# RMS norms in an interleaved attention/retention trunk: sums as rows through split products with ones

## The chip, the cores and the metric

The kernel runs on one core of one Trainium2 chip. The metric is the device time of one execution in microseconds (us); the median of three runs before the change is 2588.68 us (2587.34 to 2588.96). The engines are named as in the profile: PE is the matrix engine (PEld its weight loads), DVE the vector engine, ACT the scalar engine, POOL the GpSimd engine, SP the queue that issues most DMAs.

## The reference

Two layers, each a token mixer and a feed-forward block, every one behind an RMS norm and added to the residual; a last RMS norm ends it. x is 1 x 1024 tokens x 1024 features, float32.

```
def rmsnorm(x, g):
    y = x * rsqrt(mean(x * x, axis=-1, keepdims=True) + EPS)      # EPS = 1e-6
    return y * g

for i in range(2):
    h = rmsnorm(x, norm_mix[i])
    x = x + (forgetting_attention(h) if i == 0 else retention(h))
    h = rmsnorm(x, norm_ffn[i])
    x = x + swiglu(h)                   # (silu(h @ Wg) * (h @ Wu)) @ Wo, d_ff = 2816
return rmsnorm(x, final_norm)
```

The forgetting attention has 8 heads of 128 and a causal softmax with a decay bias. The retention has 4 heads with 256 query/key and 512 value features; its output y of every head and token is normalised before a gate: (y - mean(y)) * rsqrt(var(y) + EPS), over the head's 512 features, then times silu(g), then the output projection.

## The kernel before, in words

**Layout.** Everything is kept transposed: features on the 128 partitions, tokens in the free dimension, in two halves of 512 tokens (`HALF`). A float32 operand of a product is split into a high part, cast by ACT, and a low part, the rest, subtracted by DVE (`split`, L97 to L99); a product is then three matmuls hi*hi, hi*lo, lo*hi (`mm_u`, L101 to L108; `Products.run`, L645 to L647). The feed-forward layers, the projections of retention and part of the output projections run in a seven-product scheme on 2 x 2 blocks (`Products`, `in_turn`, `paired_out`), the operand sums (`T1` to `T4`) of which are made beforehand: `Combos` holds them in SBUF, `Stored` puts those of the feed-forward activations into DRAM (`ac...`) and fetches them back (`landed`, L496: a DMA on SP's queue straight into the low part's buffer, then a split there).

**The norms.** `Norm` accumulates the squares of the 8 feature tiles into `acc` (128 x 512 for each half; each row of it still holds one partition's share). What remains is a sum over the partitions. `colsum` (L156) takes `acc` as the stationary operand, 128 tokens at a time, against one column of a tile of ones: tokens land on partitions, four columns for a half. On these columns of 4 elements `rsqrt` (L142) takes ACT's root, DVE's reciprocal and one Newton step. To multiply tiles whose tokens lie in the free dimension, `rows` (L162) then broadcasts each column over all partitions, by a matmul of the column, repeated 128 times, with the identity. `rms` (L169) does both for the two halves and copies the result to `R` (128 x 1024). Both kinds of matmul are plain float32 ones, and each stands in the trace as two instructions. All their results, and the next column sum, go through one bank of PSUM, `ms`.

`rms` is called four times: before the attention (its columns also scale the values and keys), in each feed-forward layer's first use of R (L835) and in the first gate product of retention (L976; its columns make `kap` and `rho`, the factors of keys and outputs with their decays). `finish` (L1130) normalises a retention block of one head and one half, eight times in all: column sum of `acc`, small operations with `rho`, `rsqrt`, `rows`, then four output tiles times that row block, a gate for head 0, and the stores to `zd`. The final norm (L873 to L892) is done in three pieces of 512, 256 and 256 tokens, each ending in `colsum`, `rsqrt`, `rows`, eight multiplies and eight stores.

**Order.** The program is written for a scheduler that orders each engine's instructions in program order as priority, moving a later one ahead when earlier ones are not ready; each engine then runs its list strictly in that order. In retention the scores of the next block are made while the present one is weighted with its values: `scores` (L1080) ends in DVE steps (L1100, L99, L1105) whose results `weighted` (L1109) multiplies one block later. Pools bound how far work can run ahead: 16 tiles `y` of 128 x 512, five staging tiles `st` of 128 x 1024, six pairs `wh`/`wl` of split weights, seven PSUM banks for products and the bank `ms`.

**The joints of the feed-forward layer.** While the last of the 22 gate products runs, `coming` makes each finished block of products fetch operands of the first stored group (`FROM_COMBOS`); while the last product of group 0 runs, those of group 1 are fetched the same way (`FROM_STORED`). The start of the kernel loads four weight tiles of the first head's keys (256 KB), then the first x tiles, then the rest.

Of the kernel before, what the change touches and what calls it, by code (L numbers as in the profile page):

```python
# [37 lines left out]
def trunk(ctx, tc, nc, d, out):  # L38
# [12 lines left out]
    nc.scalar.dma_start(gains, d["gains"])  # L51
    R = cp.tile([P, S], F32, tag="R", name="R")
    cnt = [0]
# [47 lines left out]
    def mm_u(ps, wts, acts, h, cols=slice(0, H), first=True, last=True):  # L101
        n = len(wts)
        for k in range(n):
            wh, wl = wts[k]
            xh, xl = (t[:, cols] for t in acts[k][h])
            nc.tensor.matmul(ps, wh, xh, start=(first and k == 0), stop=False)  # L106
            nc.tensor.matmul(ps, wh, xl, start=False, stop=False)  # L107
            nc.tensor.matmul(ps, wl, xh, start=False, stop=(last and k == n - 1))  # L108
# [53 lines left out]
    def rows(col, mp, mtag, nb=4):  # L162
        ps = mp.tile([P, H], F32, tag=mtag, name=nm("rw"))
        for b in range(nb):
            nc.tensor.matmul(ps[:, b * P:(b + 1) * P], col[:, b:b + 1].to_broadcast([P, P]), ident,
                             start=True, stop=True)
        return ps

    def rms(norm, mp, mtag, halves=(0, 1)):  # L169
        rc = small([P, TB], "rcol", 2)  # L170
        for h in halves:
            ps = colsum(norm.acc[h], mp, mtag)
            v = small([P, 4], "rv")
            nc.vector.tensor_scalar(v, ps[:, 0:4], 1.0 / D, EPS, op0=ALU.mult, op1=ALU.add)
            rsqrt(v, 4, rc[:, 4 * h:4 * h + 4])
        for h in halves:
            ps = rows(rc[:, 4 * h:4 * h + 4], mp, mtag)
            nc.scalar.copy(R[:, HALF[h]], ps)
        return rc
# [5 lines left out]
    with ExitStack() as fs:  # L185
# [13 lines left out]
        wk0, wk1 = wtile(d["fox_qk"][1], 4), []  # L199
        for kt in range(KT):  # L200
            xs = []
            for h in range(2):
                t = half("t", 9)
                nc.sync.dma_start(t, d["xT"][:, kt, HALF[h]])
                xs.append(t)
            fed = norm.feed(kt, xs)
            x0.append(xs)
            for at, w, idx, k in (0, wk0, 1, 4), (1, wk1, 3, 0), (3, wk1, 3, 4):
                if kt == at:
                    w += wtile(d["fox_qk"][idx][:, k * P:], 4)  # L210
# [225 lines left out]
        rc = rms(norm, mp, "ms")  # L436
# [59 lines left out]
    def landed(pool, src):  # L496

        hi, lo = units(pool)
        nc.sync.dma_start(lo.bitcast(F32), src)
# [47 lines left out]
    FROM_COMBOS = {"S2": ("B11", "T1", "T2"), "S3": ("B21", "T3"), "S4": ("T4", "B22")}  # L547
# [3 lines left out]
    class Stored:  # L551


        def __init__(self, name, pools):
            self.pools = pools
# [114 lines left out]
    def in_turn(srcs, X, use, coming=None):  # L670
# [3 lines left out]
        for i in range(n):  # L674
# [7 lines left out]
            nxt = Products(srcs[i + 1], X, coming if i == n - 2 else None).open() if i < n - 1 else None  # L682
# [145 lines left out]
    def ffn(i, X, nrm, xold, xnew, last, nw, pools):  # L828
        ad = [dp.tile([P, S], F32, tag=f"ad{i}_{f}", name=f"ad{i}_{f}") for f in range(16, FT)]
        stored = [Stored(f"ac{i}_{g}_", pools) for g in range(2)]  # L830
        even = []

        def gated(f, c11, c12, c21, c22):
            if f == 0:
                rms(nrm, mp, "ms")  # L835
# [7 lines left out]
            if f < 16:  # L843
# [10 lines left out]
        in_turn([nw if f == 0 and nw else d["ffn_in"][i, f] for f in range(FT)], X, gated,  # L854
                (stored[0], FROM_COMBOS))
# [17 lines left out]
        for c0, c1 in ((0, 512), (512, 768), (768, 1024)):  # L873
# [3 lines left out]
            for n in range(KT):  # L877
                u = y[n][h][:, cs]
                ps = mm_ps()
                mm_u(ps[:, :wid], ws[n], acts, h, cs)  # L880
                nc.vector.tensor_tensor(u, ps[:, :wid], u, op=ALU.add)
                norm.square(h, u, cs, n == 0)
                nc.scalar.activation(u, u, AF.Copy, scale=gains[:, 4, n:n + 1])
                us.append(u)
            nb = wid // P
            ps = colsum(norm.acc[h][:, cs], mp, "ms", nb)
            v = small([P, nb], "rv")
            nc.vector.tensor_scalar(v, ps[:, 0:nb], 1.0 / D, EPS, op0=ALU.mult, op1=ALU.add)
            ps = rows(rsqrt(v, nb), mp, "ms", nb)
            for n in range(KT):  # L890
                nc.vector.tensor_tensor(us[n], us[n], ps[:, :wid], op=ALU.mult)
# [82 lines left out]
    def gates(p, c11, c12, c21, c22):  # L974
        if p == 0:
            rcs.append(rms(nrm, mp, "ms"))  # L976
# [33 lines left out]
    rho = small([P, RET_HEADS, TB], "rho", 1)  # L1010
    rho2 = small([P, RET_HEADS, TB], "rho2", 1)
    for h in range(RET_HEADS):
        nc.vector.tensor_tensor(kap[:, h, :], gpn[:, 0, h, :], r2, op=ALU.mult)
        nc.vector.tensor_tensor(rho[:, h, :], gpn[:, 1, h, :], rc, op=ALU.mult)
    nc.vector.tensor_tensor(rho2, rho, rho, op=ALU.mult)
# [114 lines left out]
    def finish(h, ib, yps):  # L1130
# [12 lines left out]
        cs = colsum(acc, mp, "ms")  # L1143
        var = small([P, 4], "yv")
        rs = slice(4 * ib, 4 * ib + 4)
        nc.vector.scalar_tensor_tensor(var, cs[:, 0:4], 1.0 / 512, rho2[:, h, rs], op0=ALU.mult, op1=ALU.mult)
        nc.vector.tensor_scalar(var, var, EPS, None, op0=ALU.add)
        r = rsqrt(var, 4)
        fac = small([P, 4], "yf")
        nc.vector.tensor_tensor(fac, r, rho[:, h, rs], op=ALU.mult)  # L1150
        fb = rows(fac, mp, "ms")
# [137 lines left out]
```

## Time and profile before

| | before |
|---|---|
| median of three runs | 2588.68 us |
| the profiled execution's own time | 2588.64 us |
| its span | 2586.9 us |
| PE busy | 2560.8 us, 12808 matmuls |
| DVE busy | 1839.0 us, 3131 instructions |
| ACT busy | 1228.3 us, 2320 instructions |
| POOL busy | 170.6 us, 147 instructions |
| TensorE clock granted | 0.998 |

The span is the time from the first to the last recorded instruction of the program. Rows of a line (L159 and so on) give the number of instructions, then shortest, median and longest duration in ns, first and last start in us, and shapes. A timeline row is start, duration, engine, line, operation, out<-in, and what ended an idle time before it. A row of a window gives its length and, for PE, PEld, DVE, ACT and POOL, busy us and instructions; then the clock, the DMA engines' share and GB/s. A wait's row gives who waited for whom: us in total, times, longest. Matmul durations hold their latency and overlap; what one costs PE is read from the next one's start.

### The profile page before, as it was taken

The page shows a single profiled execution, that of the slowest core. Times are in us where ns is not written, and L with a number is a line of the kernel's source. Part 1 is how long each engine was busy: PE and PEld are TensorE (multiplying, and loading weights), DVE is VectorE, ACT ScalarE, POOL GpSimd, SP SyncE. Part 2 cuts the span into 40 slices and gives each one's busy share as a digit, 9 for nine tenths or more (in the row PEclk, how much of TensorE's full clock was granted, in tenths as well). Part 3 has the DMA queues.
Part 4 walks back from the last instruction along what each step waited for, and adds up shares of the span by engine and source line. Part 5 has one row for each costly group of instructions (what it writes and reads, how often), then busy time and mean ns, then how long its engine had stood idle before and what let it go on. Part 6 is the DMA issues. An engine that isn't in the chain of part 4 may idle for free.

```text
span 2586.9 us, 35264 instructions
## 1 busy us (share of the span) xinstructions
PE 2560.8 (99%) x12808; PEld 2182.2 (84%) x12808; DVE 1839.0 (71%) x3131; ACT 1228.3 (47%) x2320; POOL 170.6 (7%) x147
## 2 busy tenths in 40 slices
PE   9999999999999999999999999999999999999998
PEld 8889887888888878889898989898888888888888
DVE  6798888966666678886656576785567666668784
ACT  6566656543333454554343435662354333335543
POOL 0143323000000000001000010000000000000000
PEclk9999999999999999999999999999999999999999
DMA  3111142432332345533332325555522333325541
GB/s 130 45 58 58 58 147 93 152 106 94 114 106 94 122 155 176 166 116 115 102 118 98 110 98 167 184 191 193 202 98 82 110 98 107 103 90 186 175 143 66
DMA packets 145759, 312.13 MB, mean 121 GB/s; under 512 B 16560, under 2 KB 29616, under 8 KB 145584
## 3 DMA queue, kind: packets, MB, share of 16 engines
q1 hardware_dynamic: 144864, 309.33, 35.9%
q8 instruction: 100, 1.64, 0.3%
q14 instruction: 75, 0.61, 0.1%
q10 hardware_dynamic: 720, 0.55, 0.1%
HBM read 217.54 MB, written 92.27 MB: 120 GB/s over the span
## 4 chain that ended last, share of the span: by engine, by line
PE 93%; DVE 2%; DMA 2%; issue 2%; ACT 1%; POOL 0%; SPq 0%; DVEq 0%; POOLq 0%; ACTq 0%
PE mm L645 18%; PE mm L647 18%; PE mm L646 18%; PE mm L106 7%; PE mm L107 7%; PE mm L108 7%; PE mm L765 2%; PE mm L763 2%; PE mm L764 2%; PE mm L256 1%; PE mm L257 1%; PE mm L258 1%; DMA b<-ac_T 1%; PE mm L1116 1%; PE mm L1117 1%
## 5 line engine op out<-in xcount | busy, mean ns | idle before, releaser
L645 PE MATMUL mm<-b,wh 128*128 128x512 f32 x2128 | 826.7, 390 | 2.7 <-ACT b L98 2.7
L646 PE MATMUL mm<-b,wh 128*128 128x512 f32 x2128 | 827.9, 389 | 0.0
L647 PE MATMUL mm<-b,wl 128*128 128x512 f32 x2128 | 825.2, 389 | 0.0
L98 ACT CAST wh<-st 128x512 fp32r<-128x512 f32 (+1 forms) x449 | 276.6, 617 | 499.2 <-PE mm L646 298.3
L645 PEld LDWEIGHTS mm<-b,wh 128*128 128x128 f32 x2128 | 399.4, 188 | 86.5 <-ACT b L98 4.0
L647 PEld LDWEIGHTS mm<-b,wl 128*128 128x128 f32 x2128 | 399.5, 188 | 83.2 <-DVE wl L99 0.4
L646 PEld LDWEIGHTS mm<-b,wh 128*128 128x128 f32 x2128 | 399.6, 188 | 82.1
L99 DVE TENSOR_TENSOR wl<-st,wh 128x512 fp32r<-128x512 f32 (+1 forms) x449 | 318.6, 713 | 180.3 <-ACT wh L98 177.9
L98 ACT CAST wh<-s 128x512 fp32r<-128x512 f32 x252 | 156.5, 622 | 298.5 <-PE mm L646 270.6
L106 PE MATMUL mm<-b,wh 128*128 128x512 f32 x736 | 286.8, 393 | 7.8 <-ACT b L126 5.5
L107 PE MATMUL mm<-b,wh 128*128 128x512 f32 x736 | 287.4, 391 | 1.7 <-DVE b L99 1.7
L108 PE MATMUL mm<-b,wl 128*128 128x512 f32 x736 | 287.4, 391 | 0.0
L99 DVE TENSOR_TENSOR wl<-s,wh 128x512 fp32r<-128x512 f32 x252 | 180.2, 717 | 89.6 <-ACT wh L98 85.5
L106 PEld LDWEIGHTS mm<-b,wh 128*128 128x128 f32 x736 | 138.9, 189 | 37.3 <-ACT b L126 6.2
L107 PEld LDWEIGHTS mm<-b,wh 128*128 128x128 f32 x736 | 138.9, 189 | 29.5 <-DVE b L99 2.2
L108 PEld LDWEIGHTS mm<-b,wl 128*128 128x128 f32 x736 | 138.8, 189 | 28.4
L764 PE MATMUL mm<-wl,b 128*128 128x256 f32 x448 | 126.6, 283 | 0.0
L763 PE MATMUL mm<-wh,b 128*128 128x256 f32 x448 | 126.2, 283 | 0.0
L765 PE MATMUL mm<-wh,b 128*128 128x256 f32 x448 | 126.2, 283 | 0.0
L597 DVE TENSOR_TENSOR s<-st 128x512 f32<-128x512 f32 x84 | 58.2, 692 | 67.8 <-DMA st<-ffn_in 28.8
L98 ACT CAST b<-b 128x512 fp32r<-128x512 f32 x112 | 67.7, 620 | 71.9 <-DMA b<-ac_B 39.2
L99 DVE TENSOR_TENSOR b<-b,b 128x512 fp32r<-128x512 f32 x112 | 75.5, 688 | 33.0 <-ACT b L98 32.6
(500 smaller groups left out, 4019.7 us busy)
## 6 DMA issues: line engine op xcount, KB each, us to landing
st<-ffn_in SPq DMA_DIRECT2D x88, 512.0 KB, 3.5
st<-ffn_out_pairs SPq DMA_DIRECT2D x32, 512.0 KB, 3.6
b<-ac_T SPq DMA_DIRECT2D x64, 256.0 KB, 5.8
ac_T<-t SPq DMA_DIRECT2D x48, 256.0 KB, 2.4
b<-ac_B SPq DMA_DIRECT2D x48, 256.0 KB, 5.0
st<-fox_qk SPq DMA_DIRECT2D x32, 256.0 KB, 2.7
xo<-xd SPq DMA_DIRECT2D x32, 256.0 KB, 3.0
ac_B<-t SPq DMA_DIRECT2D x32, 256.0 KB, 2.4
```

The source lines that it names most:

```text
L98: nc.scalar.copy(hi, src)
L99: return nc.vector.tensor_tensor(lo, src, hi.bitcast(F32), op=ALU.subtract)
L106: nc.tensor.matmul(ps, wh, xh, start=(first and k == 0), stop=False)
L107: nc.tensor.matmul(ps, wh, xl, start=False, stop=False)
L108: nc.tensor.matmul(ps, wl, xh, start=False, stop=(last and k == n - 1))
L597: nc.vector.tensor_tensor(self.s1, self.a21, self.a22, op=ALU.add)
L645: nc.tensor.matmul(ps, hi[:, js], th, start=first and j == 0, stop=False, skip_group_check=True)
L646: nc.tensor.matmul(ps, hi[:, js], tl, start=False, stop=False, skip_group_check=True)
L647: nc.tensor.matmul(ps, lo[:, js], th, start=False, stop=(j == 3), skip_group_check=True)
L763: nc.tensor.matmul(o, th[:, tk], hi[:, js], start=f, stop=False, skip_group_check=True)
L764: nc.tensor.matmul(o, th[:, tk], lo[:, js], start=False, stop=False, skip_group_check=True)
L765: nc.tensor.matmul(o, tl[:, tk], hi[:, js], start=False, stop=(j == 3), skip_group_check=True)
```

## The change

Row sums take the place of column sums and broadcasts wherever no columns are needed. `acc` is split like any operand and multiplied by a 128 x 128 tile of ones, in two fast matmuls of up to 512 columns; every partition then holds the sum of every token. The reciprocal root is taken on the full rows: ACT's root, DVE's reciprocal and a Newton step of three DVE operations.

```diff
-    ones = cp.tile([P, P], F32, tag="ones", name="ones")
-    nc.gpsimd.memset(ones, 1.0)
+    onesr = cp.tile([P, P], F32R, tag="ones", name="ones")
+    ones = onesr.bitcast(F32)
...
+    nc.vector.tensor_scalar(gains, gains, float(D) ** 0.5, None, op0=ALU.mult)
...
+    def row_sums(*accs):
+        n = accs[0].shape[-1]
+        ps = mp.tile([P, H], F32, tag="ms", name=nm("sm"))[:, :n]
+        for i, acc in enumerate(accs):
+            hi, lo = wh_wl(n)
+            split(hi, lo, acc)
+            nc.tensor.matmul(ps, onesr, hi, start=(i == 0), stop=False)
+            nc.tensor.matmul(ps, onesr, lo, start=False, stop=(i == len(accs) - 1))
         return ps
+    def row_rsqrt(r, ps, q):
+        nc.scalar.activation(q, ps, AF.Sqrt, bias=deps)
+        nc.vector.reciprocal(q, q)
+        nc.vector.scalar_tensor_tensor(r, ps, D * EPS, q, op0=ALU.add, op1=ALU.mult)
+        nc.vector.scalar_tensor_tensor(r, r, -0.5, q, op0=ALU.mult, op1=ALU.mult)
+        nc.vector.scalar_tensor_tensor(r, r, 1.5, q, op0=ALU.add, op1=ALU.mult)
+    def rms(norm, columns):
+        rc = small([P, TB], "rcol", 2) if columns else None
+        for h in range(2 if columns else 0):
...
+        for h in range(2):
+            row_rsqrt(R[:, HALF[h]], row_sums(norm.acc[h]), yu("q"))
```

`columns` is true for the calls before the attention and in retention. The mean's factor 1/D moves into the gains, which are scaled once by the root of D. In `finish` the factor of decay and norm comes as rows: R is squared and inverted after the last gates, EPS over the squared decay is written to DRAM in token order (`ed`) and loaded as a broadcast row; five of the steps run on POOL:

```diff
+    for h in range(2):
+        r = R[:, HALF[h]]
+        nc.vector.tensor_tensor(r, r, r, op=ALU.mult)
+        nc.vector.reciprocal(r, r)
...
+        fb = yu("fb")
+        row = ed[h].rearrange("(o b) p -> o (b p)", o=1)
+        nc.sync.dma_start(fb, row[:, HALF[ib]].to_broadcast([P, H]))
+        nc.gpsimd.tensor_tensor(fb, fb, R[:, HALF[ib]], op=ALU.mult)
+        nc.vector.scalar_tensor_tensor(fb, row_sums(acc), 1.0 / 512, fb, op0=ALU.mult, op1=ALU.add)
+        q = yu("q")
+        nc.scalar.activation(q, fb, AF.Sqrt)
+        nc.vector.reciprocal(q, q)
+        nc.gpsimd.tensor_tensor(fb, fb, q, op=ALU.mult)
+        nc.gpsimd.tensor_tensor(fb, fb, q, op=ALU.mult)
+        nc.gpsimd.tensor_scalar(fb, fb, -0.5, 1.5, op0=ALU.mult, op1=ALU.add)
+        nc.gpsimd.tensor_tensor(fb, fb, q, op=ALU.mult)
         for vt in range(4):
             nc.vector.tensor_tensor(ys[vt], ys[vt], fb, op=ALU.mult)
```

The final norm's last piece puts the last feature tile's residual into PSUM first and lets the products add to it; its square is a second operand of the row sum, beside `acc`:

```diff
+                if c1 == S and n == KT - 1:
+                    nc.scalar.copy(ps, u)
+                    mm_u(ps, ws[n], acts, h, cs, first=False, free=True)
+                    sq = sp.tile([P, H], F32, tag="sc", name=nm("sq"), bufs=4)[:, :wid]
+                    nc.scalar.activation(sq, ps, AF.Square)
+                    sums = row_sums(norm.acc[h][:, cs], sq)
+                    nc.scalar.activation(u, ps, AF.Copy, scale=gains[:, 4, n:n + 1])
...
+            r = R[:, c0:c1]
+            row_rsqrt(r, sums, sp.tile([P, H], F32, tag="sc", name=nm("q"), bufs=4)[:, :wid])
             for n in range(KT):
-                nc.vector.tensor_tensor(us[n], us[n], ps[:, :wid], op=ALU.mult)
+                nc.vector.tensor_tensor(us[n], us[n], r, op=ALU.mult)
```

The loads of the stored sums change too. `FROM_COMBOS` and the `coming` of `in_turn` are gone. Group 0 is staged through two `st` tiles for each sum, on SP's queue; group 1 lands as before, but from POOL's queue. At the start one weight tile is loaded ahead of x in place of four:

```diff
-                self.t[n] = [landed(self.pools[n], self.d[n][:, j * H:(j + 1) * H]) for j in range(4)]
+                if not self.staged:
+                    self.t[n] = [landed(self.pools[n], self.d[n][:, j * H:(j + 1) * H], nc.gpsimd) for j in range(4)]
+                    return self.t[n]
+                self.t[n] = []
+                for i in range(2):
+                    st = sp.tile([P, 1024], F32, tag="st", name=nm("st"), bufs=5)
+                    nc.sync.dma_start(st, self.d[n][:, i * 1024:(i + 1) * 1024])
+                    self.t[n] += [bsplit(self.pools[n], st[:, HALF[j]]) for j in range(2)]
...
-        wk0, wk1 = wtile(d["fox_qk"][1], 4), []
+        wk0, wk1 = wtile(d["fox_qk"][1], 1), []
```

More of the change, by code (lines that the diff above doesn't have):

```diff
@@ L105, in mm_u @@
             xh, xl = (t[:, cols] for t in acts[k][h])
[L106 to L108 removed]
+            nc.tensor.matmul(ps, wh, xh, start=(first and k == 0), stop=False, skip_group_check=free)
+            nc.tensor.matmul(ps, wh, xl, start=False, stop=False, skip_group_check=free)
+            nc.tensor.matmul(ps, wl, xh, start=False, stop=(last and k == n - 1), skip_group_check=free)
     HALF = (slice(0, H), slice(H, S))
@@ L435, in trunk @@
                     norm.square(h, x0[kt][h])
-        rc = rms(norm, mp, "ms")
+        rc = rms(norm, True)
         tri = const("tri", [P, P])
```

85 lines of the change are left out of this document (34 added, 51 removed).

## The prediction

> **What bounds the kernel now.** I read the page's head and busy line first, then its chain of waits.
>
> ```profile
> span 2586.9 us, 35264 instructions
> PE 2560.8 (99%) x12808; PEld 2182.2 (84%) x12808; DVE 1839.0 (71%) x3131; ACT 1228.3 (47%) x2320; POOL 170.6 (7%) x147
> PE 93%; DVE 2%; DMA 2%; issue 2%; ACT 1%; POOL 0%; SPq 0%; DVEq 0%; POOLq 0%; ACTq 0%
> ```
>
> The matrix engine (PE) is busy for 99% of the span, and 93% of the chain that ends last is PE. So a matmul taken away is time saved, as long as no other engine becomes late for PE. The view of PE's waits has little that could be won besides:
>
> ```profile
> PE mm L106 <- ACT b L126: 5.5, 1, 5.5
> PE mm L645 <- ACT b L98: 2.7, 3, 1.5
> ```
>
> The first is the start (nothing to multiply for 5.5 us), the second the joints inside the feed-forward layers. Busy time of matmuls overlaps, so their price is read from starts. This is PE's timeline around a column sum (L159) and around a row broadcast (L165):
>
> ```profile
> 504.17 0.39 PE L646 MATMUL mm<-b,wh 128*128 128x512 f32 x1
> 504.40 0.95 PE L159 MATMUL cs<-ones,acc 128*128 128x1 f32 x8
> 505.21 0.49 PE L647 MATMUL mm<-b,wl 128*128 128x512 f32 x1
> 505.53 0.40 PE L645 MATMUL mm<-b,wh 128*128 128x512 f32 x1
> ...
> 516.00 1.05 PE L165 MATMUL rw<-ident,rcol 128*128 128x128 f32 x8
> 516.81 0.48 PE L647 MATMUL mm<-b,wl 128*128 128x512 f32 x1
> ```
>
> A 512-column split product takes 0.23 us from start to start (504.17 to 504.40). Eight column-sum instructions take 0.81 us to the next start, and that one runs 0.09 long (0.32 to its follower): 0.90, or 0.1125 each. Eight broadcasts show the same 0.81, and I take 0.1125 for them too.
>
> **PE's account.** How many there are, by line:
>
> ```profile
> L159 PE MATMUL cs<-ones,acc x80: 164/250/250, 40.0 to 2577.4; 128*128 128x1 f32 x80
> L159 PE MATMUL cs<-ones,yacc x64: 164/250/250, 1633.4 to 1772.3; 128*128 128x1 f32 x64
> L165 PE MATMUL rw<-ident,rcol x64: 271/275/275, 47.5 to 1966.4; 128*128 128x128 f32 x64
> L165 PE MATMUL rw<-ident,yf x64: 270/275/275, 1640.7 to 1779.9; 128*128 128x128 f32 x64
> L165 PE MATMUL rw<-ident,rs_d x16: 270/275/553, 2548.2 to 2580.0; 128*128 128x128 f32 x16
> ```
>
> These are 144 of each. Two of the four `rms` calls keep their columns (2 calls x 2 halves x 8 = 32 column sums), so 112 column sums and all 144 broadcasts go. Four of each lie in the last stretch after the last projection, which is worked out by itself; 108 + 140 = 248 by 0.1125 is 27.9 us. Added before that stretch are two split products per half: four `rms` calls with two halves (16) and eight calls of `finish` (16) at 0.23, 7.4 us; the final norm's first block two at 0.23 and its second two of 256 columns at 0.12 (rows below), 0.7. PE: 27.9 - 8.1 = 19.8 us less.
>
> **The two ends.** The start: the first weight load is a quarter as large, so the first x tile, behind it on SP's queue, comes sooner; but gains must now land and be scaled before the first feed.
>
> ```profile
> 4.76 1.36 ACT L126 ACTIVATE b<-t,gains 128x512 fp32r<-128x512 f32 x2
> DMA to landing us min/median/max: 3.4/3.4/3.4
> ```
>
> Issued at 0.7 us, gains land at 4.1; one small DVE operation later the feed may begin, at about 4.4 rather than 4.76. I take 0.3 us less (bounds 0.4 less to 0.3 more). The end:
>
> ```profile
> 2575.15 0.28 PE L107 MATMUL mm<-b,b 128*128 128x256 f32 x1
> 2575.27 0.28 PE L108 MATMUL mm<-b,b 128*128 128x256 f32 x1
> 2575.58 0.42 DVE L881 TENSOR_TENSOR 22_4457_22642<-mm,22_4457_22642 128x256 f32<-128x256 f32 x1 [0.82 <-PE mm L108]
> 2576.04 0.42 ACT L138 ACTIVATE sq<-22_4457_22642 128x256 f32<-128x256 f32 x1 [1.19 <-DVE 22_4457_22642 L881]
> 2577.06 0.58 PE L159 MATMUL cs<-ones,acc 128*128 128x1 f32 x4 [1.52 <-DVE acc L139]
> 2580.44 0.42 DVE L891 TENSOR_TENSOR 12_4372_22212<-12_4372_22212,rw 128x256 f32<-128x256 f32 x1 [1.38 <-PE rw L165]
> ```
>
> From the last product's end (2575.55) to the first output multiply are 4.9 us now. The new chain is square, copy, subtract (0.42 each with 0.04 between), two products of 0.12 with their latency (0.4 and the hand-offs 0.2), a root (0.5), a reciprocal of 256 columns, three DVE steps of 0.45, then the same multiplies. The reciprocal's price comes from two shapes:
>
> ```profile
> L283 DVE RECIPROCAL f_s<-f_s x1: 553/553/553, 61.8 to 61.8; 128x64 f32<-128x64 f32 x1
> L146 DVE RECIPROCAL rs_b<-rs_a x19: 156/178/183, 41.4 to 2578.1; 128x4 f32<-128x4 f32 x17, 128x2 f32<-128x2 f32 x2
> ```
>
> (553 - 178)/60 is 6.25 ns a column, so 256 columns are an estimated 1.75 us and 512 are 3.35. The new chain comes to 5.6 us: the end is 0.7 longer, not shorter (0.6 shorter if a wide reciprocal takes no longer than the 0.42 of an addition). The Trainium skill (VectorE: DVE Perf Modes, the fixed hardware budget) says that a reciprocal is an iterative division with a repeat count of 8; were that 8 cycles of its 0.96 GHz, an estimate by that page is 8.3 ns a column, 4.4 us for 512, and the sum would be 9 us worse (six calls in the retention, R's two, the end). The rows' slope is below that, and the sum goes by the rows.
>
> **DVE takes over what PE drops.** An `rms` call now puts two reciprocals, two subtractions and six row steps on DVE: 2 x (3.35 + 4 x 0.69) = 12.2 us. In the stretch of the first feed-forward norm:
>
> ```profile
> 505.00:525.00 20.00, 20.00 (x99) 16.84 (x99) 13.85 (x32) 8.63 (x15) 0.00 (x0) 1.00 0.24 78
> ```
>
> DVE (third number) is idle for 6 of 20 us there, and the two sums are now broadcast 11.6 us after their column sum (504.40, 516.00) without a wait of PE. I cost the four calls at nothing, with that slack as cover; if it is gone, PE meets the second half's sum while the one bank `ms` is still read: root 0.6, reciprocal 3.35, first step 0.69, up to 4.6 us a call.
>
> The retention has no such slack. From its first scores to its last:
>
> ```profile
> 1608.00:1752.00 144.00, 142.66 (x853) 129.36 (x852) 120.23 (x286) 97.42 (x215) 0.00 (x0) 1.00 0.57 187
> L1141 DVE TENSOR_TENSOR yacc<-yacc,sq x24: 682/690/694, 1626.5 to 1758.0; 128x512 f32<-128x512 f32 x24
> L1153 DVE TENSOR_TENSOR yt<-yt,rw x32: 678/681/689, 1642.2 to 1782.0; 128x512 f32<-128x512 f32 x32
> ```
>
> DVE is busy for 120.2 of 144 us. Six of the eight calls of `finish` fall into it (by the row of their column sums, 1633.4 to 1772.3, they are 20 us apart). Each loses eight small DVE operations (8 x 0.17 = 1.3) and gains a reciprocal (3.35), a subtraction and a row step (0.69 each): 3.4 more. Squaring and inverting R after the last gates adds 2 x (0.69 + 3.35) = 8.1, once. And each call now runs five operations on POOL, which did nothing here. What that does to DVE is seen where POOL rotates keys:
>
> ```profile
> 1158.51 1.29 POOL L952 TENSOR_TENSOR m<-m,m 128x512 f32<-128x512 f32 x1 [726.42 <-DMA st<-ret_v]
> 1158.88 1.47 DVE L99 TENSOR_TENSOR wl<-s,wh 128x512 fp32r<-128x512 f32 x1
> ```
>
> The DVE subtraction begun under the POOL operation took 1.47 us, 0.78 over L1141's 0.69, and ended 0.55 after POOL did. So one call costs DVE between nothing (no POOL operation meets a DVE operation with two SBUF inputs) and 5 x 0.78 = 3.9. I take two meetings of five, 1.6, because DVE has a sixth of its time idle and long reciprocals and PSUM reads in it, under which POOL may hide; both ends are kept.
>
> Demand on DVE: 120.2 + 8.1 + 6 x (3.4 + 1.6) = 158.3 us. PE needs 144 less 6 x (0.90 + 0.90 - 0.46) = 136. DVE is 22.3 over. Cover: DVE's score splits are ready well before PE's weighted products use them. For head 2, first block:
>
> ```profile
> 1682.03 0.61 DVE L1105 SCALAR_TENSOR_TENSOR wl<-mm,kap,wh 128x384 fp32r<-128x384 f32 x1
> 1682.83 0.48 DVE L1105 SCALAR_TENSOR_TENSOR wl<-mm,kap,wh 128x256 fp32r<-128x256 f32 x1
> 1688.07 0.39 PE L1115 MATMUL mm<-wh,b 128*128 128x512 f32 x1
> 1692.78 0.33 PE L1115 MATMUL mm<-wh,b 128*128 128x384 f32 x1
> ```
>
> The first split ends at 1682.6 and is used at 1688.1, the second at 1683.3 and 1692.8: 5.4 and 9.5 us, 7 in the mean. One call's work may also trail behind PE (it holds six of 16 `y` buffers): some 5 us of it and 2.8 of multiplies, say 7. Cover 14; PE waits 8.3 us. With 0 meetings it waits for nothing (148.7 against 136 and 14), with all five 22.
>
> **The loads.** `coming` no longer fetches group 0 while the last gate product runs; group 1 moves from SP's queue to POOL's, away from SP's weight loads and stores, and behind POOL's own operations (none in this stage).
>
> ```profile
> b<-ac_T SPq DMA_DIRECT2D x64, 256.0 KB, 5.8
> 905.47 6.18 DMA b<-ac_T
> ```
>
> Today these loads sit on the chain at the joint (905 to 912), and PE waits 2.7 us at such places in all. Group 0 now goes in halves through five `st` buffers shared with the weights, on SP's queue; what queues behind a full buffer there is the next weight block, for which ACT and DVE, then PE, wait. I cost the move at 0: a store is long done when its load starts, so the scheduler may place the loads as early as now. Bounds: 2.7 less, to 7.5 more for each layer (a load 6.18, a cast 0.62, a subtraction 0.69 with nothing in front). POOL's queue issues no load in this trace; its issue I bound by the same two numbers. R's broadcast rows (`fb`) and the four `ed` stores are on SP as well; they depend on nothing late, so 0, at worst a landing of 6 us that delays only a finish.
>
> **Sum**, against the profiled execution's 2588.64 us (span 2586.9; the median of runs is 2588.68): -19.8 - 0.3 + 0.7 + 8.3 = -11.1, which is 2577.5 us. Only 0.2% (5.2 us) can be told from no change.
>
> **Rivals.** *The cover holds.* The scheduler finds an order in which POOL's operations fall under DVE's reciprocals and idle time: PE loses nothing in the retention, -19.4, 2569.2 us. For it: the leads of 5 to 9 us; against it: 120 of 144 us are taken already.
>
> *DVE and POOL exclude each other in the retention* (slower). All five operations of each call hold up DVE: 120.2 + 8.1 + 6 x 7.3 = 172, 36 over PE's 136, less 14 is 22 of waiting: +2.6, 2591; with a cover of 5.4 alone 30.6, +11, 2600. It decides from 19.4 us of waiting on, 3.45 a call, which is 4.4 meetings of five. For it: most of DVE's work there reads two SBUF operands, as L1141 does, and the output multiplies (L1153), which read PSUM now, will too; against it: only full collision reaches it. The Trainium skill (SBUF — State Buffer, Who interferes with whom) states this as a rule: the two share a port pair as an exclusive lock, and a DVE operation with two SBUF inputs blocks wholly against a POOL operation that reads SBUF. The 1.47 us row agrees.
>
> *The joints starve.* Group 0's first loads come only when first used: 7.5 us in each layer, +3.9 with the forecast's other terms, 2592.5; in one layer alone 2585. For it: loads land after 5.8 us; against it: nothing in the loads' data forbids an early issue.
>
> *It does less than it says:* the wide products do not run at the split products' pace; at twice 0.23 the 32 of them cost 7.4 us more, 2585. Against it: they are of the same shape and type as L646's.
>
> **How the numbers follow.** Chances: forecast 0.38 (its own range 2572 to 2585), cover holds 0.33, exclusion 0.18, joints 0.08, less than it says 0.03. Range: 2566 (2569.2 with the joints' 2.7 us gone) to 2598 (most of the exclusion's 2591 to 2600). Faster by over 0.2%, under 2583.5: 0.33 of the cover and 0.26 of the forecast, 0.59. Within 0.2%: 0.12 of the forecast, 0.04 of the exclusion, 0.04 of the last two, 0.20. Slower: 0.14 of the exclusion and 0.07 of joints and the rest, 0.21.
>
> **What would show it.** PE has 256 - 40 = 216 matmuls fewer; the broadcasts are gone, and two products per half stand in its place with starts 0.23 apart. Reciprocals of 512 columns at 3.35 us (0.7 would bring the end in and free DVE). DVE's busy time in the retention rises to 95% or more, with subtractions of about 1.4 us beside POOL; PE's waits there name DVE. If they name DVE for under 3 us, the cover held; over 19, exclusion. At the joints, waits for `b` or `st` loads of over 3 us show starving. A wait of PE for `ms` or for DVE's R after a norm would show that the slack at 505 was no cover. The prediction is wrong if the time lies outside the range, or if the retention keeps its pace and the time is lost elsewhere.

## The result, and the profile after

The changed kernel takes 2633.59 us (median of 4 runs, 2631.73 to 2636.83) against 2588.82 us for the kernel before beside it (4 runs, 2587.34 to 2590.37). The ratio is 1.017, 95% interval 1.0158 to 1.0182: 44.8 us slower. The prediction was 2577.5 us, range 2566 to 2598; the time lies outside it, on the other side of no change.

The head of the page of the changed kernel, its busy line and its chain of waits:

```profile
span 2630.0 us, 34904 instructions
PE 2559.7 (97%) x12592; PEld 2170.5 (83%) x12592; DVE 1944.3 (74%) x3107; ACT 1245.8 (47%) x2338; POOL 261.0 (10%) x245
PE 87%; DVE 6%; issue 3%; DMA 2%; ACT 1%; POOL 0%; DVEq 0%; POOLq 0%; SPq 0%; ACTq 0%
```

PE has the 216 matmuls fewer that were forecast, and yet its busy time is the same: what went out as work came back as matmuls that are spread thinner. DVE's share of the chain rises from 2% to 6%.

To place the loss I take, for every matmul, the time from its start to the next start, less the median of that for its shape (227 ns for 512 columns, 120 for 256, in both kernels), and sum these excesses. I call the sum PE's lost time, give it for a stretch of the trace, and use it for every kernel below; "the start" is the first 50 us, "the retention" 1550 to 1900 us. Up to the last product the two traces then balance:

| us | before | after | difference | forecast |
|---|---|---|---|---|
| first matmul | 5.5 | 4.9 | -0.6 | -0.3 |
| matmuls at their medians | 2548.4 | 2528.9 | -19.5 | -19.8 |
| lost, start | 3.1 | 11.9 | +8.8 | 0 |
| lost, retention | 2.3 | 54.4 | +52.1 | +8.3 |
| lost, all else | 15.9 | 15.6 | -0.3 | 0 |
| last product's start to the span's end | 11.6 | 14.3 | +2.7 | +0.7 |
| span | 2586.9 | 2630.0 | +43.1 | -11.1 |

So the gain on PE came, almost to the tenth, and the retention took it back more than twice over. The windows of the changed kernel there (length, then PE, PEld, DVE, ACT and POOL, the granted clock, DMA) and the waits of PE from 1600 to 1860 us:

```profile
1608.00:1620.00 12.00, 7.89 (x39) 6.01 (x37) 12.00 (x19) 7.12 (x17) 0.00 (x0) 1.00 0.53 175
...
1692.00:1704.00 12.00, 6.33 (x19) 4.67 (x20) 11.81 (x21) 5.94 (x15) 1.93 (x1) 0.72 0.69 216
1704.00:1716.00 12.00, 12.00 (x64) 10.67 (x63) 12.00 (x17) 7.53 (x15) 7.58 (x5) 1.00 0.15 48
...
1608.00:1800.00 192.00, 153.72 (x793) 132.25 (x792) 181.36 (x272) 110.78 (x235) 51.94 (x36) 0.91 0.50 161
```

```profile
PE sm L175 <- ACT wh L104: 9.4, 1, 9.4
PE sm L176 <- DVE wl L105: 5.9, 2, 3.8
PE mm L1156 <- DVE wl L105: 5.6, 1, 5.6
PE mm L1129 <- ACT yt L1175: 4.1, 1, 4.1
PE mm L1129 <- DVE wl L1145: 3.6, 1, 3.6
```

DVE is busy for 181.4 of 192 us and PE for 153.7. These are the windows of the kernel before:

```profile
1608.00:1620.00 12.00, 11.68 (x69) 10.45 (x68) 9.40 (x24) 7.39 (x18) 0.00 (x0) 1.00 0.47 149
1608.00:1800.00 192.00, 190.66 (x1082) 169.70 (x1081) 142.82 (x333) 107.45 (x234) 0.00 (x0) 1.00 0.56 184
```

Of the 54.4 us lost, 42 lie in 16 places where PE lost over 0.35 us at once (the waits of the view above are among them). Another 9 are 54 matmuls that ran while the granted clock stood at half, and 3 are small pieces. Half clock was granted for 37.5 us in all, in five stretches. PE stood waiting for some 15 of them, and a matmul at half clock loses only half of its time there, so the time lost by it is read from the matmuls and not from the mean clock of 0.91. The slow matmuls are seen after the longest wait, in PE's timeline:

```profile
1797.76 0.80 PE L175 MATMUL sm<-wh,ones 128*128 128x512 f32 x1 [9.36 <-ACT wh L104]
1798.35 0.73 PE L112 MATMUL mm<-b,wh 128*128 128x512 f32 x1
1798.88 0.63 PE L113 MATMUL mm<-b,wh 128*128 128x512 f32 x1
1799.30 0.63 PE L112 MATMUL mm<-b,wh 128*128 128x512 f32 x1
```

Starts come down to 0.42 us apart where they were 0.23, for some microseconds after each long gap. The Trainium skill (TensorE: Matmul & The Clock Gate, Part 1) states that half clock follows an idle window of about 3.4 us and gives 426.7 ns for 512 columns. The trace agrees on the 0.42 us; half clock also followed a shorter wait here, of 2.0 us (`no_recip` below, clock 0.50 from 1694.2 to 1697.6 us).

Where the loss lies matters too. The last score split of the stage starts at 1771.8 us:

```profile
L1145 DVE SCALAR_TENSOR_TENSOR wl<-mm,kap,wh x24: 341/483/620, 1619.7 to 1771.8; 128x384 fp32r<-128x384 f32 x8, 128x256 fp32r<-128x256 f32 x8, 128x128 fp32r<-128x128 f32 x8
```

Up to it PE loses 32.8 us, behind it 21.5: there the last calls of `finish` meet the first weights of the output projection.

The groups of DVE's work from 1608 to 1800 us show both suspects, the reciprocals and the additions and subtractions that POOL holds up (L1181 took 0.69 us before):

```profile
L105 DVE TENSOR_TENSOR b<-st,b 128x512 fp32r<-128x512 f32 x40 | 32.3, 826 | 0.0
L1181 DVE TENSOR_TENSOR yacc<-yacc,sq 128x512 f32<-128x512 f32 x24 | 25.6, 1066 | 1.1 <-ACT sq L1180 0.8
L1190 DVE RECIPROCAL q<-q 128x512 f32<-128x512 f32 x7 | 23.5, 3352 | 1.4 <-ACT q L1189 1.4
L1046 DVE RECIPROCAL R<-R 128x512 f32<-128x512 f32 x2 | 6.7, 3348 | 0.0
```

Summed over all of DVE's operations there, each against the usual duration of its line and shape, some 25 us are excess, beside 36 POOL operations: 0.70 us for each. It falls on operations with two operands in SBUF. One that reads PSUM kept its duration, although eight of its 32 ran beside POOL (shortest, median, longest in ns):

```profile
L1140 DVE SCALAR_TENSOR_TENSOR atd<-mm,kap,mask x32: 252/343/361, 1614.2 to 1775.7; 128x128 f32<-128x128 f32 x32
```

### The profile page after: what moved, and what is told of

It reads as the page before. It is cut to its first block, busy times and chain, and to the rows that moved or that the text cites. A ratio compares the mean times of both kernels' runs of the same rounds, so it can differ in the third digit from the quotient of the medians.

```text
span 2630.0 us, 34904 instructions
## 1 busy us (share of the span) xinstructions
PE 2559.7 (97%) x12592; PEld 2170.5 (83%) x12592; DVE 1944.3 (74%) x3107; ACT 1245.8 (47%) x2338; POOL 261.0 (10%) x245
## 4 chain that ended last, share of the span: by engine, by line
PE 87%; DVE 6%; issue 3%; DMA 2%; ACT 1%; POOL 0%; DVEq 0%; POOLq 0%; SPq 0%; ACTq 0%
PE mm L668 18%; PE mm L669 18%; PE mm L670 18%; PE mm L112 7%; PE mm L113 7%; PE mm L114 7%; PE mm L788 2%; PE mm L786 2%; PE mm L787 2%; DVE b L105 1%; DMA st<-vd 1%; DVE b L1066 1%; PE mm L274 1%; PE mm L275 1%; PE mm L273 1%
## 5 line engine op out<-in xcount | busy, mean ns | idle before, releaser
L104 ACT CAST wh<-st 128x512 fp32r<-128x512 f32 (+4 forms) x450 | 276.8, 617 | 530.4 <-PE mm L669 329.6
L105 DVE TENSOR_TENSOR wl<-st,wh 128x512 fp32r<-128x512 f32 (+4 forms) x450 | 319.4, 713 | 183.4 <-ACT wh L104 180.2
L516 POOL DMA_DIRECT2D b<-ac_B x24 | 13.5, 561 | 1181.9 <-PE mm L669 1179.8
L104 ACT CAST b<-st 128x512 fp32r<-128x512 f32 (+1 forms) x160 | 91.9, 610 | 62.6 <-DVE st L824 20.2
L105 DVE TENSOR_TENSOR b<-st,b 128x512 fp32r<-128x512 f32 (+1 forms) x160 | 109.6, 710 | 15.0 <-ACT b L104 14.4
```

Of the source, the lines that this page charges most:

```text
L104: nc.scalar.copy(hi, src)
L105: return nc.vector.tensor_tensor(lo, src, hi.bitcast(F32), op=ALU.subtract)
```

## The experiments

The theory (A): the new `finish` makes DVE late for PE, by the reciprocals and by the exclusion between DVE and POOL. Rivals: the exclusion alone (B); the row sum, by its place in PE's list (C2) or because its split takes one of the six pairs `wh`/`wl` that the score splits and the next weights use (C1); the loads, clock or other norms (D). All times but those of the last two kernels are single runs; the kernel before beside them took 2586.7 to 2588.4 us.

**ret_old**, the old `finish` in the changed kernel:

```diff
-        fb = yu("fb")
...
-        nc.gpsimd.tensor_tensor(fb, fb, q, op=ALU.mult)
+        cs = colsum(acc, mp, "ms")
...
+        fb = rows(fac, mp, "ms")
```

> The change with the finish of before in the retention (column sum, narrow root, broadcast; R is neither squared nor inverted there, no POOL steps); the other norms, the loads and the ends stay as changed. Theory A (the new finish costs about 52 us because DVE has more work and is held up by POOL): 2633.6 - 52 = about 2581, with PE's waits in 1600 to 1850 us back at some 2 to 3 us. Rival D (the loss comes from the loads, the clock or the other norms, and falls on the retention only by its place): 2625 or more. The start's loss of about 9 us should stay under both.

2588.6 us; lost in the retention 1.4, at the start 10.9. PE's waits in the retention are gone (one row is left):

```profile
PE mm L1152 <- DVE wl L1141: 0.3, 1, 0.3
```

The retention's loss is that of `finish`; D falls. The time is 8 us above the expectation because the old `finish` also brings its matmuls back (10.7 us), which I had left out of that sum.

**ret_new**, only the new `finish` in the kernel before (the reverse diff):

> The kernel before with only the retention's finish as changed (R squared and inverted, rows of the broadcast decay, row sums, five steps on POOL); all other norms, loads and ends as before. Theory A: PE loses about 52 us of waiting in the retention and gains 8 x (1.80 - 0.46) = 10.7 us of matmuls less: 2588.7 + 52 - 11 = about 2630. Rival D: within 5 us of 2578 (the gain of the matmuls alone). If only the whole change together loads the engines enough, it lies between, at 2590 to 2610.

2643.2 us; lost in the retention 55.9, and at the start 16.5. The first number is as expected. The second is not: the norm at the start is the old one here. It led to ret_new_edrow, below.

**no_recip, no_pool, neither.** The wide reciprocals left out (the root is then scaled by a constant), the POOL steps left out, both:

```diff
-        nc.vector.reciprocal(q, q)
```
```diff
-        nc.gpsimd.tensor_tensor(fb, fb, R[:, HALF[ib]], op=ALU.mult)
...
-        nc.gpsimd.tensor_tensor(fb, fb, q, op=ALU.mult)
-        nc.gpsimd.tensor_tensor(fb, fb, q, op=ALU.mult)
-        nc.gpsimd.tensor_scalar(fb, fb, -0.5, 1.5, op0=ALU.mult, op1=ALU.add)
-        nc.gpsimd.tensor_tensor(fb, fb, q, op=ALU.mult)
```

> The change, with the wide reciprocals of the retention left out: the eight of the finish and R's two (the output isn't the reference's; every other instruction is there). Takes about 7 x 3.36 + 2 x 3.35 = 30 us from DVE between 1600 and 1800 us. Theory A (DVE's total work is the bound): PE waits about 30 us less, about 2604. Rival B (the exclusion between DVE and POOL is the cause, the reciprocals fall into gaps): at most 5 us less, 2628 or more. Rival C (the row sum's place in PE's order or its share of the six split pairs): about 3.4 us per call that stands ahead of the row sum's follower only, not the sum itself, so 2620 to 2630.

> The change, with the five POOL steps of each finish left out (the decay row is taken as loaded, the root isn't refined; the output isn't the reference's); reciprocals and row sums stay. DVE's excess beside POOL was about 25 us over 1608 to 1800 us, and the chain from a row sum to the output multiplies is 5.6 us shorter. Theory A (total work of DVE, of which the exclusion is about half of the excess): about 25 us less, 2606 to 2610. Rival B (exclusion alone): nearly all, 2580 to 2586. Rival C (place of the row sum, split pairs): 2625 or more, since the sum's inputs don't pass POOL.

> The change, with both the retention's wide reciprocals and the five POOL steps of each finish left out (the output isn't the reference's); row sums by split products with ones stay in their place. Theory A (DVE's work plus exclusion): about 55 us off DVE, PE's waits in the retention back below 5 us: about 2581. Rival C (the row sum itself: its place in PE's list, or that it takes one of the six split pairs): the loss stays, 2610 or more.

Lost in the retention, after 54.4: without reciprocals 32.5 (2616.5 us), without POOL steps 41.7 (2624.9), without both 16.0 (2596.4). So 22 for the ten reciprocals, 13 for the POOL steps, 38 together: nearly additive. B alone falls, A holds, but each part was smaller than I expected and 16 us are neither. PE's waits in `neither` name the larger part of the rest:

```profile
PE sm L175 <- ACT wh L104: 7.1, 1, 7.1
PE mm L1103 <- DVE wl L1144: 1.4, 1, 1.4
```

**own_pair, neither_own.** The retention's row sums split into two free tiles of their own, in the changed kernel and in `neither`:

```diff
-            hi, lo = wh_wl(n)
+            hi, lo = own or wh_wl(n)
...
+    own += [yq.tile([P, H], F32R, tag="q", name=nm(t)) for t in ("oh", "ol")]
     prepare(0)
```

> The change, with the row sums of the retention split into two tiles of their own (free tiles of the cosine pool) in place of one of the six weight pairs; the work is the same. Theory A: same time within 5 us, 2629 to 2638. Rival C1 (the sum's pair shortens the lead of the score splits by one pair): 20 to 50 us less, 2585 to 2613. The start keeps its pair and its loss of 9 us.

> The change without the retention's wide reciprocals and without the POOL steps of finish (the output isn't the reference's), and with the retention's row sums split into two tiles of their own in place of a weight pair. Without reciprocals and POOL steps PE still lost 16.0 us in the retention, 7.1 of it where a row sum's pair stands ahead of the output projection's weights. Theory C1 for that rest (the pair): down to 2 to 6 us, 2582 to 2586. Rival A (the split's own work on ACT and DVE, and the sum's place in PE's list): no change, 2593 to 2598.

Lost 43.8 (2624.4 us) against 54.4, and 6.2 (2592.2) against 16.0: some 10 us either way, less than the 20 to 50 of C1 but real, and A's "same within 5" was wrong. It is not the lead of the score splits that C1 spoke of: up to the last score split own tiles saved nothing in the changed kernel (36.0 against 32.8), behind it the loss fell from 21.5 to 7.9, and in `neither` from 9.2 to nothing. What the shared pair holds up is the output projection's first weights: in `neither` their first cast comes at 1762.6 us, right behind the last row sum's at 1762.1, in `neither_own` at 1756.2. In `neither_own` the row sum waits for next to nothing:

```profile
PE sm L177 <- ACT oh L104: 0.3, 1, 0.3
```

Its total came 6 us above the expectation although the retention's loss is at its upper end: the start lost 16.8 us in this run and 14.7 in `neither`, and the stretches besides lost some 4 us more. That is why I judge by the stretch.

**late**, the second half of `finish` written after the second weighted block of the next stage:

```diff
+            if dg == 1 and late:
+                finish2(*late)
         a = an
-        finish(h, ib, yps)
+        late = (h, ib, *finish(h, ib, yps))
```

> The change, with the second half of each finish (from the decay row's load on) written after the second weighted block of the next stage, so that its row sum stands later in PE's list; the work is the same. Theory A: DVE's work stays, so most of the loss stays, 2615 to 2636; only waits at the row sums themselves (11.7 and 5.9 us in the profile after) can go. Rival C2 (the row sum stands too early in PE's list and blocks it): nearly all of it back, 2580 to 2595.

2662.6 us, lost 79.6: slower than anything expected. PE still waits at the row sums:

```profile
PE sm L175 <- ACT wh L104: 18.4, 4, 9.4
```

C2 in this form (the sum stands too early) falls: a later place made those waits longer. Why the rest of the stage suffers as well was not settled.

**on_dve**, the five POOL steps on DVE (`nc.gpsimd` becomes `nc.vector` in `finish`):

> The change, with the five POOL steps of each finish on DVE. DVE gains 8 x (4 x 0.69 + 0.40) = 25 us of its own work and loses the 25 us of excess beside POOL; the chain of a finish is 7.3 - 3.2 = 4 us shorter. Theory A: near the changed kernel, 2625 to 2640. Rival B (exclusion costs more than its excess in durations): clearly faster, under 2615.

2631.2 us, lost 49.5 against 54.4. As A has it: on POOL the steps cost PE no less than on DVE itself.

**pool_off, pool_on, recip_off, recip_on.** What was open: do reciprocals and POOL steps cost by DVE's time, or as links in the chain from the row sum to the output multiplies? On the base `neither_own` (6.2 lost), each was put in the chain (on) and into a spare tile that nobody reads (off):

```diff
         nc.scalar.activation(q, fb, AF.Sqrt, scale=1e-36)
+        nc.gpsimd.tensor_tensor(scr, scr, q, op=ALU.mult)
+        nc.gpsimd.tensor_tensor(scr, scr, q, op=ALU.mult)
+        nc.gpsimd.tensor_scalar(scr, scr, -0.5, 1.5, op0=ALU.mult, op1=ALU.add)
+        nc.gpsimd.tensor_tensor(scr, scr, q, op=ALU.mult)
```
```diff
         nc.scalar.activation(q, fb, AF.Sqrt, scale=1e-36)
+        nc.vector.reciprocal(scr, fb)
```

> Base: row sums with tiles of their own, no wide reciprocals in the retention, no POOL steps (2592.2 us, 6.2 us lost by PE in the retention; the output isn't the reference's there and here). Added: the five POOL steps of each finish, at their place and on the same operands, but into a spare tile that nobody reads. If POOL costs by holding up DVE (exclusion): 8 to 14 us more, about 2600 to 2606. If it costs only as a part of the chain: under 3 us more, up to 2595.

> The same base with the five POOL steps in the chain, as in the change (the wide reciprocals of the retention still left out). By the earlier runs (reciprocals left out: 32.5 us lost; the own tiles took 10 us off) about 22 us lost, 16 more than the base: 2606 to 2609. Exclusion alone: the same as with the spare tile, within 3 us; chain: 8 us or more above it.

> The same base with one reciprocal of 128x512 in each finish, on the same operand and at its place in DVE's order, but into a spare tile that nobody reads (output not the reference's). If the reciprocals cost by the time they take from DVE, in order: 8 x 3.36 = 27 us of DVE, 12 to 25 us more than the base, 2604 to 2617. If they cost only as a part of the chain: under 3 us more. Since DVE runs its list in order, the next step of the chain waits behind it in both forms; a difference to the next run over 4 us would speak for the chain through ACT, POOL and the stores.

> The same base with the eight reciprocals of finish in the chain, R's two still left out, no POOL steps (the decay row as loaded, no refinement). Demand: the same as with the spare tile within 4 us, 2604 to 2617. By the earlier run without POOL steps (41.7 us lost with ten reciprocals and the shared pair): 41.7 - 10 - 2 x 3.35 = about 25 us lost, 19 more than the base, 2611.

| | time, us | lost in the retention | more than the base | DVE's time added |
|---|---|---|---|---|
| pool_off | 2612.9 | 29.2 | 23.0 | 33 excess, 40 operations |
| pool_on | 2606.6 | 27.3 | 21.1 | 23 excess, 40 operations |
| recip_off | 2605.3 | 26.5 | 20.3 | 8 x 3.35 = 26.8 |
| recip_on | 2603.0 | 22.8 | 16.6 | 26.8 |

Off costs no less than on. It is the time taken from DVE, by the exclusion as by the reciprocals, and not the longer chain. For the reciprocals this excludes only the part of the chain outside DVE, since DVE runs its list in order. `pool_off` cost more than the 8 to 14 us expected, with more excess on DVE than in the chain. A microsecond of DVE's time costs PE 0.6 to 0.9.

**ret_new_edrow**, `ret_new` with the decay rows turned by TensorE and stored in rows of 512 bytes:

```diff
-        nc.sync.dma_start(ed[h].rearrange("b p -> p b"), e[:, h, :])
+        nc.tensor.transpose(pt[:TB, :P], e[:, h, :], ident)
...
+        nc.sync.dma_start(ed[h], er)
```

> The kernel before with only the finish as changed, but the rows of the decay turned by TensorE and stored in rows of 512 bytes in place of single elements of 4 bytes. Theory E (the four element-wise stores, which start at about 21 us because they hang on nothing but the decays, hold the DMA queues for some 15 us while the value weights should land; PE lost 16.5 us in the first 50 us, 9.9 in one wait): 2643.2 - 10 to 13, 2630 to 2633, and 3 to 6 us lost at the start. Rival (the start's loss there is of another kind, an order of loads or splits): 2640 or more.

2630.5 us; lost at the start 3.1 in place of 16.5. The stores of `ed` hang on nothing but the decays, so they were issued at 21 us, 1600 us ahead of their use. First the DMA view of `ret_new` from 14 to 60 us (KB each, us to landing), then its windows, then those of `ret_new_edrow`:

```profile
ed<-rho SPq DMA_DIRECT2D x4, 4.0 KB, 16.4
```
```profile
20.00:30.00 10.00, 10.00 (x46) 8.27 (x45) 5.65 (x12) 4.52 (x9) 0.00 (x0) 1.00 1.23 5
30.00:40.00 10.00, 1.83 (x14) 1.58 (x12) 0.00 (x0) 0.00 (x0) 0.00 (x0) 0.73 1.13 42
```
```profile
20.00:30.00 10.00, 10.00 (x45) 8.27 (x45) 8.35 (x15) 7.48 (x15) 0.00 (x0) 1.00 0.35 109
30.00:40.00 10.00, 10.00 (x83) 9.89 (x81) 6.73 (x11) 6.52 (x11) 0.00 (x0) 1.00 0.15 52
```

The last two columns are the DMA engines' share and GB/s. A packet's whole time counts where it starts, so the share can pass 1. From 20 to 30 us the engines are fully taken at 5 GB/s, while the value weights should land, and PE then works 1.8 of 10 us.

**start_old**, the old `finish` and, in the first norm, row factors by broadcasts; **best**, the end of before as well:

```diff
+            if first:
+                nc.scalar.copy(R[:, HALF[h]], rows(rc[:, 4 * h:4 * h + 4], mp, "ms"))
+            else:
                 row_rsqrt(R[:, HALF[h]], row_sums(norm.acc[h]), yu("q"))
```

> The change with two parts undone: the retention's finish of before, and in the norm before the attention the row factors by broadcasts of its columns, as before (no row sums there). Theory A (the row sums of the start take two of the six split pairs ahead of the value weights, so PE meets the column sum before it has other products; 10.9 us of lost time in the first 50 us with the old finish, 3.1 in the kernel before): 2588.6 - 7.8 = about 2581, with no wait of PE at the column sum. Rival (the start is lost through the single key tile that is loaded first, or the loads' order): 2587 or more.

> As the run with the old finish and the old start, and with the end of before as well (column sums and broadcasts in the final norm, no residual put into PSUM first). Row sums stay in the two feed-forward norms and in the first gates' norm, where DVE has slack; the loads stay as changed. The last product's end to the end of the span was 13.0 us with the changed end, 11.3 in the kernel before, for 0.8 us of matmuls: theory A about 2581 - 1.7 + 0.7 = 2580, below both kernels. If the row sums of the feed-forward norms or the loads lost time somewhere that only the whole shows: 2586 or more.

start_old 2583.2 us (10 runs, 2581.5 to 2588.1), ratio to before 0.9982, interval 0.9973 to 0.9991; lost at the start 2.4. best 2582.6 us (9 runs, 2581.7 to 2584.4), ratio 0.9978, interval 0.9968 to 0.9987: 0.2% faster than the kernel before, a small gain outside the interval. It keeps row sums in three of the four `rms` calls. Both are 2 to 3 us above the expectation, and start_old against best is not told apart.

## Why the prediction was wrong

**What held.** PE's account: -19.8 forecast, -19.5 measured. The reciprocal of 512 columns, estimated at 3.35 us from two narrow shapes, took 3.35. By the Trainium skill's repeat count of 8 (VectorE: DVE Perf Modes, the fixed hardware budget), taken as 8 cycles, the estimate was 4.4. The joints: no starving, all else -0.3. The `rms` calls of the feed-forward layers cost no waits, as their slack promised.

**The step that failed: "Cover 14; PE waits 8.3 us".** The retention lost 52.1 us more than before, for four reasons, which overlap and so do not add up exactly. The sign that the prediction named for exclusion, waits for DVE of over 19 us, came (23 us of PE's waits from 1600 to 1860 name DVE), but it could not tell POOL from the reciprocals: without POOL steps 41.7 us were lost still.

First, the cover. I averaged the lead of DVE's splits at one place (head 2, first block: 5.4 and 9.5 us) and added 7 us that may trail, and subtracted the sum from the demand of the whole stage. A lead can only be used where it stands. R's squaring and inverting falls on the first blocks. There the first low part has no lead at all in the kernel before; PE waits for it:

```profile
1612.30 0.62 DVE L1105 SCALAR_TENSOR_TENSOR wl<-mm,kap,wh 128x384 fp32r<-128x384 f32 x1
1612.97 0.50 PE L1116 MATMUL mm<-wl,b 128*128 128x512 f32 x1 [0.32 <-DVE wl L1105]
```

In the window 1608 to 1620 above DVE is busy for 12.00 of 12 us and PE for 7.89 (9.40 and 11.68 before). In the 50 us that begin 10 us ahead of R's squaring PE lost 7.7 to 8.5 us in the seven kernels that have R's reciprocals, and 1.3 to 5.3 in the seven that leave them out (2.1 and 1.9 in recip_on and recip_off, which have the others). And the added operations cost PE 0.6 to 0.9 of their own time at a DVE share that I had called slack: `no_recip` lost 32.5 us with DVE busy for 162.7 of 192 us.

```profile
1608.00:1800.00 192.00, 168.93 (x883) 145.44 (x882) 162.69 (x283) 116.06 (x244) 59.65 (x40) 0.95 0.56 184
```

Second, the meetings with POOL. I took two of five at 0.78 us, 1.6 a call, "because DVE has a sixth of its time idle". Measured: 0.70 for each POOL operation, 3.5 a call. PSUM reads did run under POOL at no cost (L1140 above), but that hid little. With 3.5 a call the prediction's own sum has DVE 33.7 us over PE's need, and 32.8 were lost up to the last score split, as if nothing had been covered. That the two meet so closely is in part luck: for `no_pool` the same sum is 12.7 over, and 23.6 were lost there. In the changed kernel's timeline four DVE operations in a row meet POOL:

```profile
1774.01 1.78 DVE L1181 TENSOR_TENSOR yacc<-yacc,sq 128x512 f32<-128x512 f32 x1
1775.21 1.74 POOL L1192 TENSOR_TENSOR fb<-fb,q 128x512 f32<-128x512 f32 x1
...
1775.98 1.52 DVE L105 TENSOR_TENSOR b<-st,b 128x512 fp32r<-128x512 f32 x1
...
1777.42 1.63 DVE L824 TENSOR_TENSOR st<-st,st 128x1024 f32<-128x1024 f32 x1
1778.06 2.12 POOL L1194 TENSOR_TENSOR fb<-fb,q 128x512 f32<-128x512 f32 x1
1778.97 1.76 DVE L105 TENSOR_TENSOR b<-st,b 128x512 fp32r<-128x512 f32 x1
```

The rival of exclusion had the mechanism and the price (3.45 a call was its point of decision), but kept a cover and so gave 2591 to 2600. The Trainium skill's rule (SBUF — State Buffer, Who interferes with whom: an exclusive lock) spoke against this change; `pool_off` and `on_dve` bear it out in the stage's time.

Third, the stage's end and the pair. The demand sum stopped at 1752 us with six of the eight calls, and for what trails behind it PE was to pay nothing; 21.5 us were lost behind the last score split. `row_sums` takes a `wh`/`wl` pair of the six, and there the output projection's weights queue behind it. I did not cost this; it is 10 us in the retention (`own_pair`, `neither_own`).

Fourth, the clock: of the 54 us, 9 are matmuls at about half pace after a gap. No term of mine had it, though the first matmuls of the trace of before, from 6 to 12 us, start 0.42 us apart too.

**The start: 0.3 less forecast, 8.2 more measured** (8.8 lost, the first matmul 0.6 sooner). The first matmul did come sooner. But "they depend on nothing late, so 0" was the wrong conclusion for the `ed` stores: what depends on nothing late is issued early, here into the scarcest moment of the DMA queues. And the row sums' two pairs stand ahead of the value weights' pairs: PE meets the column sum before it has other products. In `ret_old`, which has no `ed`, the first value weights are cast at 34.5 us, behind the row sums' own casts; in the kernel before at 21.2:

```profile
33.19 0.62 ACT L104 CAST wh<-acc 128x512 fp32r<-128x512 f32 x1
34.50 1.16 ACT L104 CAST wh<-st 128x528 fp32r<-128x528 f32 x2
```
```profile
21.20 1.15 ACT L98 CAST wh<-st 128x528 fp32r<-128x528 f32 x2
```

The wait in the changed kernel and in `ret_old`:

```profile
PE cs L165 <- DVE acc L145: 3.7, 1, 3.7
```
```profile
PE cs L165 <- DVE acc L145: 3.6, 1, 3.6
```

Either cause alone loses as much at the start (10.9 with the pairs, 16.5 with `ed`) as both (11.9 in the profile after, 11.9 to 16.8 over the twelve profiles that have both); without either it is 2.4 to 3.1. I costed this `rms` call together with the feed-forward ones, from the slack at 505 us, and did not look at its own stretch.

**The end: +0.7 forecast, +2.7 measured.** The chain itself is as priced (reciprocal of 256 columns 1.75). What I left out is that the piece before it ends late too: its eight multiplies run until 2616.9, and the two additions to `acc` that the last sum needs come behind them in DVE's order.

```profile
2616.54 0.42 DVE L920 TENSOR_TENSOR 22_4465_22595<-22_4465_22595,R 128x256 f32<-128x256 f32 x1
2616.88 0.95 DVE L145 TENSOR_TENSOR acc<-acc,sq 128x256 f32<-128x256 f32 x2
```

## What to carry to other kernels

Taking matmuls from PE pays only where the engine that gets the work has room at that very place: look at the lead block by block, at its smallest, before you subtract it, follow the sum to where the stage's last work ends, and count a POOL operation beside two-input DVE work at its full price to DVE. A helper that draws on a shared ring of buffers moves everything behind it in that ring, and a store without late inputs will be issued early; look at what it meets there. Where the root on narrow columns spares the engine that wide rows would fill, as in the retention, or the columns are needed anyway, as in the first norm here, leave them.

## What the runs showed of the hardware that was not expected

- Five steps moved to POOL saved DVE nothing: 49.5 us lost with them on DVE, 54.4 on POOL; into a tile that nobody reads they still cost PE 23.0 us.
- A 4 KB store in single elements takes 14.6 us to land (median in the changed kernel; 16.4 in `ret_new`), and with four of them the DMA engines' share stood at 1.11 and 1.23 at 4 to 5 GB/s. The value weights' loads of 264 KB land in 2.9 us before, 5.1 in the changed kernel and 10.9 in `ret_new`. In the window from 14 to 60 us the changed kernel has 4698 packets under 512 bytes, the kernel before 553.
- After a gap of some microseconds matmuls of 512 columns start 0.42 us apart for a while; in the retention that was 9 of the 54 us lost. Half clock was granted for 37.5 us there, and PE stood waiting for some 15 of them.
